# DRAM sums of the second FFN weights: half pieces on ScalarE's queue, one layer in the scan and one in attention; tile sums behind plain tiles

## The chip, the core and the metric

The kernel runs on one core of a Trainium2 chip. The metric is the device time of one execution in microseconds (us); where several runs are given, their median. A profile is of one execution; its times count from the start of its span.

## What is computed

One inference step of a two-layer encoder on 1024 prompt frames and 64 frames of a running stream, 1088 columns in all, in float32:

```python
for layer in range(2):
    if layer == 0:   # Mamba-2 mixer: in-projection, short convolution, scan over chunks, gate, out-projection
        m = ssd_mixer(rmsnorm(x, nw[0]), h0, c0, *params)
    else:            # banded attention on a shared K/V of the stream after layer 0
        k, v = shared_kv(x, kv_norm_w, w_kv)
        m = band_attention(rmsnorm(x, nw[0]) @ w_q, k, v, rel_bias) @ w_o
    x = x + rmsnorm(m, nw[1])
    x = x + rmsnorm(swiglu(rmsnorm(x, nw[2]), ffn_w_in[layer], ffn_w_out[layer]), nw[3])

def swiglu(u, w_in, w_out):
    g, up = split(u @ w_in, 2)          # 1024 -> 2 x 2816
    return (silu(g) * up) @ w_out       # 2816 -> 1024
```

Outputs are the stream, the scan's and convolution's states and the new K/V rows.

## The kernel before

**Numbers and products.** Each float32 operand is split into a high part (rounded to the format that TensorE takes) and a low part, and a product is made of three matmuls (L489 to L491, L1378 to L1380, L1714 to L1716). The high part is a ScalarE copy, the low part a VectorE subtraction (`part`, L363 and L364). For some weights, those planned with `acc`, the low part is made otherwise: ScalarE writes the negated high part (L358), and a DMA of GpSimd's queue adds the weights from DRAM (L359).

**Stages.** The scan (in-projection, convolution and chunk scan, up to about 690 us), out-projection, FFN of layer 0, attention, FFN of layer 1. The loops run over weight tiles of 128 x 1024 and three slices of columns, `SL` (384, 384, 320); in the FFN over two blocks of columns.

**FFN.** Both FFN products save multiplications by Strassen's scheme in Winograd's form: seven products of blocks stand for eight, and need sums of weight blocks. For the first weights the sums are made tile by tile, next to the work: SP loads a block into `tt` (L282), a DMA of GpSimd's queue adds a second one (L288, a "tile sum"), and VectorE finishes (L330, L331); `advance` does the planning. The first 6 tile pairs of each FFN (`PGS`) are plain, without sums; the first three and the last of these pairs are `acc` tiles. `sq` is the list of tiles still to be split, in order, and a tile with the key `two` is of the seven-product kind; `aq` holds tile sums that wait for their time.

**DRAM sums.** For the second weights the sums are made once, in DRAM, long ahead of use: `weight_sums(layer)` fills `wsm_[layer]`, of shape (128, 4, 4, 1408), from `w_f2[layer]`. With a and b the two weight tiles of group g (of four), each cut into halves of n = 1408 columns, a0, a1, b0, b1, it makes z[3] = b0 + b1 and z[2] = a0 + b0, z[0] = z[3] + a0 and z[1] = a1 + z[0], in five steps: copy into z[2:4], add, copy z[3] to z[0] and a1 to z[1], add, add. Copies are DMAs of SP's queue, adds are accumulating DMAs of GpSimd's queue, all from DRAM to DRAM. The two layers' steps are chained, 40 in all, and three are issued ahead of each group of units of the scan, from the fifth group on (L1157 to L1160). FFN of layer 0 loads the sums from about 1370 us on, FFN of layer 1 from about 2700 us on (L1322).

**What sets the order.** TensorE's order is the program's. All other engines' queues are ordered by a scheduler that looks at when it thinks an instruction is ready, and at priorities; each queue then runs in order on the chip. To keep an early transfer from being moved to the front, a manual dependency places it behind another instruction of the same engine: SP's copies behind the last weight load (`W.loaded`), the sums behind `last_g`, the last halo copy of a convolution on GpSimd (L826).

**The scan's inner work.** A "unit" is one product of a weight tile with a slice, 24 matmuls. `order` lists groups of two or three weight tiles (18 groups), each run over three slices. A unit's result is scaled out of PSUM by VectorE (L798), then goes through the convolution (`Conv`: ScalarE L836, VectorE L838, ScalarE L842 to L846) or a gate. `ssd_task` runs the chunk scan for one weight tile and slice: SP loads MT and ea, rows of the decay table spread over partitions (L922, L925); VectorE subtracts (L931), ScalarE takes the exponential (L932, L933).

**Attention.** For each of eight pairs of heads j there are nine units, K, V and Q for three slices (`evk`, `evv`, `evq`), which run ahead of nine blocks of scores. `load_bias(j)` loads two bias tiles and GpSimd masks their corners (L1809, L1810); there are three buffers, so the second tile of a pair waits for the first of the pair before. GpSimd also clears the ends of K (L1826), Q (L1845) and V (L1880); K has two buffers for each head. ScalarE copies K's high part (L1829), takes the softmax's exponentials (L1928) and empties every second transposed tile (L1948).

Of the kernel before, what the change touches and what calls it, by code (L numbers as in the profile page):

```python
# [2 lines left out]

# [87 lines left out]
C_CB = 168  # L91
# [144 lines left out]
class Weights:  # L236
# [38 lines left out]
    def advance(self):  # L275
        moved = True
        while moved:
            moved = False
            while self.tq and self.tt.free():
                it = self.tq.pop(0)  # L280
                it["T"] = self.tt.get()
                self.loaded = self.nc.sync.dma_start(it["T"].rearrange("p (e k) -> p e k", e=2), it["two"][0])  # L282
                if self.behind is not None:
                    self.tc.add_manual_dep(self.loaded.ins, self.behind.ins.name, ORDER, reason="place in the order")
                self.aq.append((self.clock() + ACC_W, it))
            while self.aq and self.aq[0][0] <= self.clock():
                it = self.aq.pop(0)[1]
                self.nc.gpsimd.dma_start(it["T"], it["two"][1], accum_op=ALU.add)  # L288
# [111 lines left out]
def hybrid_kernel(  # L400
# [63 lines left out]
    def col(c):  # L464
        return pcs[:, c:c + 1]
# [123 lines left out]
            UC.put(c)  # L589


    last_g = [None]

    def weight_sums(layer):

        w2, z, n = w_f2[layer], wsm_[layer], HF * P

        def sp(x):
            tc.add_manual_dep(x.ins, W.loaded.ins.name, ORDER, reason="place in the order")

        def pool(x):
            tc.add_manual_dep(x.ins, last_g[0].ins.name, ORDER, reason="place in the order")

        steps = []
        for g in range(4):
            a, b, to = w2[2 * g], w2[2 * g + 1], z[:, g]
            steps.append((
                lambda g=g, to=to: sp(nc.sync.dma_start(to[:, 2:4, :], w2[2 * g:2 * g + 2, :, :n].rearrange("e p k -> p e k"))),
                lambda b=b, to=to: pool(G.dma_start(to[:, 2:4, :], b.rearrange("p (e k) -> p e k", e=2), accum_op=ALU.add, max_dma_last_dim=4 * n)),
                lambda a=a, to=to: (sp(nc.sync.dma_start(to[:, 0, :], to[:, 3, :])), sp(nc.sync.dma_start(to[:, 1, :], a[:, n:]))),  # L610
                lambda a=a, to=to: pool(G.dma_start(to[:, 0, :], a[:, :n], accum_op=ALU.add)),
                lambda to=to: pool(G.dma_start(to[:, 1, :], to[:, 0, :], accum_op=ALU.add)),
            ))
        for f in range(5 + 3):
            for g in range(4):
                if 0 <= f - g < 5:
                    yield steps[g][f - g]

    order = []
    for g in range(NG):  # L620
# [94 lines left out]
    with ExitStack() as es:  # L715
# [92 lines left out]
        class Conv:  # L808
# [5 lines left out]
            def __call__(self, s, ps_):  # L814
                ct = self.ct
                dst = self.dst[s] = sb2.tile([P, 384], F32, tag=self.tag, bufs=self.bufs, name=self.tag)
                raw = sb2.tile([P, 390], F32, tag="craw", bufs=4, name="craw")
                if s == 0:
                    G.memset(raw[:, 0:3], 0.0)
                else:  # L820
                    G.tensor_copy(raw[:, 0:3], self.prev[:, 0:3])
                if s < 2:
                    w_ = 384
                    scaled(raw[:, 3:387], ps_, s, 0, 384)
                    self.prev = sb2.tile([P, 4], F32, tag="halo", bufs=5, name="halo")
                    last_g[0] = G.tensor_copy(self.prev[:, 0:3], raw[:, 384:387])  # L826
                else:
                    w_ = 323
                    G.tensor_copy(raw[:, 259:262], scs[:, ct, :])
                    scaled(raw[:, 3:259], ps_, s, 0, 256)  # L830
                    scaled(raw[:, 262:326], ps_, s, 256, 64)
                    G.tensor_copy(cst[:, ct, 0:3], raw[:, 256:259])
                    G.tensor_copy(cst[:, ct, 3:6], raw[:, 323:326])

                cw = C_CW + ct * 4
                A.activation(dst[:, :w_], raw[:, 0:w_], AF.Identity, bias=col(C_CB + ct), scale=col(cw))  # L836
                for k in range(1, 4):
# [316 lines left out]
            pend[s] = [dps] * (s < 2) + box  # L1154
        finish(2)
        side[0] = pyy
        staged = chain_of(weight_sums(0), weight_sums(1))  # L1157
        for i, grp in enumerate(order):
            for _ in range(3 if i > 3 else 0):
                next(staged, lambda: None)()  # L1160
            ws = [W.get() for _ in grp]
            ev = [evac_of(*f) for f in grp]
            if len(grp) < 3:
                seq = [(i, s) for s in range(NSL) for i in range(len(grp))]
                if grp is order[0]:

                    seq = [(0, 0), (0, 1), (1, 0), (1, 1), (1, 2), (0, 2)]
            else:
                seq = [(0, 0), (1, 0), (0, 1), (0, 2), (2, 0), (1, 1), (2, 1), (1, 2), (2, 2)]
            for i, s in seq:  # L1170
                kd_, jj_ = grp[i]
                q = 3 * jj_ + s
                if kd_ == "x":
                    st.wait_for(lambda: so["C"] > q - 5)
                elif kd_ == "z":
                    st.wait_for(lambda: so["D"] > q - 3)
                elif kd_ == "C" and q >= 5:
                    g_, s_ = divmod(q - 5, 3)
                    st.wait_for(lambda: so["C"] > 3 * (4 * g_ + 3) + s_)
                unit(ws[i], u[s], SL[s][1], lambda p_: ev[i](s, p_))  # L1180
                if s == 2:
                    W.put()
        nc.sync.dma_start(cst_o, cst)
# [588 lines left out]
    with ExitStack() as es:  # L1772
# [30 lines left out]
        def load_bias(j):  # L1803

            bias = []
            for e in range(2):
                bt = late["sb3"].tile([P, WIN], F32, tag="bias", bufs=3, name="bias")
                nc.sync.dma_start(bt, bass.AP(rbrow.tensor, (2 * j + e) * 768, [[1, P], [1, WIN]]))
                G.memset(bt[0:64, 0:64], NEG)  # L1809
                G.memset(bt[64:128, 576:640], NEG)  # L1810
                bias.append(bt)
            kqv[j]["bias"] = bias

        def evk(j):
            d = kqv[j]

            def f(s, p_):
                n = SL[s][1]
                st.wait_for(lambda: ("rb", s) in done)
                kf = sb2.tile([P, 384], F32, tag="kqv", bufs=2, name="kf")  # L1820
                with tc.high_priority(HIP):
                    V.tensor_tensor(kf[:, :n], p_[:, :n], rba[s][:, :n], op=ALU.mult)
                if not d["Kt"]:
                    d["Kt"] = [sb2.tile([P, 9 * P], F32R, tag=f"K{e}", bufs=2, name=f"K{e}") for e in range(2)]
                    for Kd in d["Kt"]:
                        G.memset(Kd[:, T:].bitcast(F32), 0.0)  # L1826
                for e, Kd in enumerate(d["Kt"]):
                    hi, lo = Kd[H2[e], 384 * s:384 * s + n], Kd[H2[1 - e], 384 * s:384 * s + n]
                    A.copy(hi, kf[H2[e], :n])  # L1829
                    V.tensor_tensor(lo, kf[H2[e], :n], hi, op=ALU.subtract)  # L1830
                d["K"].add(s)
                if s:
                    a_, b_, c_ = (128, 384, 0) if s == 1 else (0, 320, 256)
                    nc.sync.dma_start(kT_o[j * P:(j + 1) * P, c_:c_ + b_ - a_], kf[:, a_:b_])
# [237 lines left out]
        st.wait_for(lambda: cur["A"] >= 3)  # L2072
        units(wq, 0, evq, (2,))
        W.put()
        for j in range(1, 8):
            if j > 1:
                load_pair(j)
# [9 lines left out]
            while left:  # L2087
# [171 lines left out]
```

## Time and profile before

| | us |
|---|---|
| median of 3 runs | 2953.83 |
| lowest, highest | 2951.97, 2958.01 |
| the profiled execution | 2944.86 |
| its span, first to last instruction | 2943.2 |

| stretch of the profile (us) | length | TensorE busy | DMA share |
|---|---|---|---|
| 850 to 900 | 50 | 50.00 | 0.76 |
| 900 to 950 | 50 | 42.75 | 0.72 |
| 1600 to 1650 | 50 | 38.79 | 0.38 |
| 1700 to 1750 | 50 | 47.24 | 0.27 |
| 2250 to 2300 | 50 | 45.69 | 0.65 |
| 2400 to 2450 | 50 | 50.00 | 0.60 |

In the profile PE is TensorE, PEld its weight loads, DVE VectorE, ACT ScalarE, POOL GpSimd and SP the engine that issues most DMAs; a q behind a name is that engine's sequencer, which waits and issues DMAs. L with a number is a line of the kernel. A row of a timeline has the start, the duration, engine, line, operation, output and inputs, and in brackets how long the engine was idle before it and what ended that. A row of busy time by stretch has busy us and count of each engine, the mean granted clock of TensorE, the share of time that the 16 DMA engines were busy, and GB/s.

### The profile page before, as it was taken

What the parts mean: (1) busy time and instruction counts of PE and PEld (TensorE: products, weight loads), DVE (VectorE), ACT (ScalarE), POOL (GpSimd) and SP (SyncE); (2) the same over time, 40 slices, a digit from 0 to 9 for tenths busy, and PEclk for the clock granted to TensorE, in tenths of its full rate; (3) what the DMA queues carried; (4) which work ended last, traced back from release to release, by engine and by line L of the source; (5) the groups of instructions that cost most, each with busy time, mean ns of one, the idle gap of its engine ahead of it and who ended that gap; (6) DMA issues with size and microseconds to landing.
All of it is one profiled execution on the core that took longest, in us unless ns stands there. A gap on an engine that the chain in (4) does not pass through costs nothing. (4 is left out here: it accounts for less than half of the span.)

```text
span 2943.2 us, 58213 instructions
## 1 busy us (share of the span) xinstructions
PE 2858.4 (97%) x22094; PEld 2810.2 (95%) x22094; DVE 2131.8 (72%) x4834; ACT 1424.9 (48%) x2616; POOL 605.3 (21%) x880
## 2 busy tenths in 40 slices
PE   8999998999999999999999899999999999999999
PEld 8998898999998999999998899999999999999998
DVE  7987786886767665676559877877768766567567
ACT  6655545554554333344345556656565333334343
POOL 1334334340220222221022000000031122221011
PEclk9999999999999999999999999999999999999999
DMA  4439677654647656577655222222368555667666
GB/s 137 129 132 240 179 206 205 182 162 140 191 143 195 160 142 161 139 213 224 191 173 164 89 65 89 77 72 76 100 202 230 144 146 151 161 188 222 194 197 193
DMA packets 261673, 471.30 MB, mean 160 GB/s; under 512 B 26256, under 2 KB 162672, under 8 KB 261392
## 3 DMA queue, kind: packets, MB, share of 16 engines
q1 hardware_dynamic: 241584, 400.40, 42.0%
q0 software_dynamic: 19808, 67.19, 13.3%
q8 instruction: 173, 2.83, 0.4%
q14 instruction: 108, 0.88, 0.1%
HBM read 381.90 MB, written 127.26 MB: 173 GB/s over the span
## 5 line engine op out<-in xcount | busy, mean ns | idle before, releaser
L489 PE MATMUL mm<-r,hl 128*128 128x384 f32 (+2 forms) x1704 | 571.4, 335 | 25.2 <-DVE zs L798 12.4
L490 PE MATMUL mm<-r,hl 128*128 128x384 f32 (+2 forms) x1704 | 552.4, 324 | 2.4 <-DVE r L1592 2.4
L491 PE MATMUL mm<-r,hl 128*128 128x384 f32 (+2 forms) x1704 | 552.1, 324 | 1.4 <-DVE hl L364 0.7
L489 PEld LDWEIGHTS mm<-r,hl 128*128 128x128 f32 x1704 | 324.1, 190 | 31.6 <-DVE zs L798 12.6
L1379 PE MATMUL px<-r,hl 128*128 128x288 f32 (+1 forms) x1184 | 348.8, 295 | 0.0
L490 PEld LDWEIGHTS mm<-r,hl 128*128 128x128 f32 x1704 | 324.2, 190 | 3.3 <-DVE r L1592 3.0
L491 PEld LDWEIGHTS mm<-r,hl 128*128 128x128 f32 x1704 | 323.3, 190 | 2.0 <-DVE hl L364 1.1
L1380 PE MATMUL px<-r,hl 128*128 128x288 f32 x1056 | 313.3, 297 | 4.6 <-DVE hl L364 4.5
L1378 PE MATMUL px<-r,hl 128*128 128x288 f32 x1056 | 311.6, 295 | 0.0
L364 DVE TENSOR_TENSOR hl<-raw,hl 128x1024 fp32r<-128x1024 f32 (+2 forms) x171 | 195.1, 1141 | 92.9 <-ACT hl L363 92.3
L1714 PE MATMUL po<-r,hl 128*128 128x288 f32 (+1 forms) x856 | 246.7, 288 | 0.0
L1715 PE MATMUL po<-r,hl 128*128 128x288 f32 (+1 forms) x856 | 246.7, 288 | 0.0
L1716 PE MATMUL po<-r,hl 128*128 128x288 f32 (+1 forms) x856 | 246.6, 288 | 0.0
L1379 PEld LDWEIGHTS px<-r,hl 128*128 128x128 f32 x1184 | 223.7, 189 | 0.0
L363 ACT CAST hl<-raw 128x1024 fp32r<-128x1024 f32 (+2 forms) x171 | 165.7, 970 | 110.2 <-PE po L1716 41.4
L1378 PE MATMUL px<-rx,hl 128*128 128x256 f32 x768 | 213.8, 278 | 1.6 <-DVE u L1393 1.6
L1380 PE MATMUL px<-rx,hl 128*128 128x256 f32 x768 | 213.9, 279 | 0.3 <-DVE hl L364 0.3
L1380 PEld LDWEIGHTS px<-r,hl 128*128 128x128 f32 x1056 | 200.1, 189 | 5.4 <-DVE hl L364 5.3
L1378 PEld LDWEIGHTS px<-r,hl 128*128 128x128 f32 x1056 | 200.2, 190 | 0.0
L1379 PE MATMUL px<-rx,hl 128*128 128x256 f32 x640 | 178.3, 279 | 0.0
L1714 PEld LDWEIGHTS po<-r,hl 128*128 128x128 f32 x856 | 161.5, 189 | 0.0
L1716 PEld LDWEIGHTS po<-r,hl 128*128 128x128 f32 x856 | 160.9, 188 | 0.3 <-DVE hl L364 0.3
(385 smaller groups left out, 8019.2 us busy)
## 6 DMA issues: line engine op xcount, KB each, us to landing
raw<-in_w_f_dram SPq DMA_DIRECT2D x64, 512.0 KB, 4.9
tt<-in_w_f_dram SPq DMA_DIRECT2D x44, 512.0 KB, 4.1
tt<-in_w_f_dram POOLq DMA_DIRECT2D x44, 512.0 KB, 6.6
raw<-in_w_in_dram SPq DMA_DIRECT2D x40, 512.0 KB, 4.4
MT<-ascr SPq DMA_DIRECT2D x48, 384.0 KB, 4.9
raw<-in_w_so_dram SPq DMA_DIRECT2D x32, 512.0 KB, 3.8
r<-hscr SPq DMA_DIRECT2D x56, 288.0 KB, 3.9
wsum<-in_w_f_dram SPq DMA_DIRECT2D x8, 1408.0 KB, 10.1
```

The costliest lines, as they stand in the source:

```text
L363: self.nc.scalar.copy(h, v)
L364: (eng or self.eng or self.nc.vector).tensor_tensor(lo, v, h, op=ALU.subtract)
L489: PE.matmul(ps[:, :n], h_, xh, start=(first and i == 0), stop=False)
L490: PE.matmul(ps[:, :n], h_, xl, start=False, stop=False)
L491: PE.matmul(ps[:, :n], l_, xh, start=False, stop=(last and i == nk - 1))
L1378: PE.matmul(ps, wh, ah[:, k, :], start=(k == 0), stop=False)
L1379: PE.matmul(ps, wh, al[:, k, :], start=False, stop=False)
L1380: PE.matmul(ps, wl, ah[:, k, :], start=False, stop=(k == 3))
L1714: PE.matmul(ps, wh, xh, start=(k0 > 0 and i == ks[0]), stop=False)
L1715: PE.matmul(ps, wh, xl, start=False, stop=False)
L1716: PE.matmul(ps, wl, xh, start=False, stop=(k0 == 0 and i == ks[-1]))
```

## The change

The tile sums of `advance` are issued only when the next tile to be split is of the seven-product kind. `weight_sums` makes eight pieces for a layer, each half of a group's columns (704), in six steps; up to three pieces are in work in turn. The copies go out on ScalarE's queue, behind `last_a`: the last convolution's first instruction in the scan, the last copy of K's high part in attention. In the scan one step of layer 0's sums follows each unit of the first two slices, from the second group of units on; in attention one step of layer 1's sums follows each unit from j = 1 on, with the sums placed behind the last bias memset. The DRAM transfers' bytes stay the same in all.

```diff
-            while self.aq and self.aq[0][0] <= self.clock():
+            while self.aq and self.aq[0][0] <= self.clock() and 'two' in self.sq[0]:
                 it = self.aq.pop(0)[1]
                 self.nc.gpsimd.dma_start(it["T"], it["two"][1], accum_op=ALU.add)
...
-    last_g = [None]
+    last_g, last_a = [None], [None]
...
-        steps = []
-        for g in range(4):
-            a, b, to = w2[2 * g], w2[2 * g + 1], z[:, g]
-            steps.append((
-                lambda g=g, to=to: sp(nc.sync.dma_start(to[:, 2:4, :], w2[2 * g:2 * g + 2, :, :n].rearrange("e p k -> p e k"))),
-                lambda b=b, to=to: pool(G.dma_start(to[:, 2:4, :], b.rearrange("p (e k) -> p e k", e=2), accum_op=ALU.add, max_dma_last_dim=4 * n)),
-                lambda a=a, to=to: (sp(nc.sync.dma_start(to[:, 0, :], to[:, 3, :])), sp(nc.sync.dma_start(to[:, 1, :], a[:, n:]))),
-                lambda a=a, to=to: pool(G.dma_start(to[:, 0, :], a[:, :n], accum_op=ALU.add)),
-                lambda to=to: pool(G.dma_start(to[:, 1, :], to[:, 0, :], accum_op=ALU.add)),
-            ))
-        for f in range(5 + 3):
-            for g in range(4):
-                if 0 <= f - g < 5:
-                    yield steps[g][f - g]
+        c = n // 2
+
+        def behind(x, last):
+            tc.add_manual_dep(x.ins, last[0].ins.name, ORDER, reason="place in the order")
+
+        def copy(to, x):
+            behind(A.dma_start(to, x), last_a)
+
+        def add(to, x):
+            behind(G.dma_start(to, x, accum_op=ALU.add), last_g)
+
+        def steps(g, o):
+            a, b, to = w2[2 * g], w2[2 * g + 1], z[:, g, :, o:o + c]
+            yield lambda: copy(to[:, 2:4, :], w2[2 * g:2 * g + 2, :, o:o + c].rearrange("e p k -> p e k"))
+            yield lambda: add(to[:, 2:4, :], b.rearrange("p (e k) -> p e k", e=2)[:, :, o:o + c])
+            yield lambda: copy(to[:, 0, :], to[:, 3, :])
+            yield lambda: copy(to[:, 1, :], a[:, n + o:n + o + c])
+            yield lambda: add(to[:, 0, :], a[:, o:o + c])
+            yield lambda: add(to[:, 1, :], to[:, 0, :])
+
+        pieces = [steps(g, o) for g in range(4) for o in (0, c)]
+        live = []
+        while pieces or live:
+            while pieces and len(live) < 3:
+                live.append(pieces.pop(0))
+            for p_ in list(live):
+                f = next(p_, None)
+                if f is None:
+                    live.remove(p_)
+                else:
+                    yield f
...
-                A.activation(dst[:, :w_], raw[:, 0:w_], AF.Identity, bias=col(C_CB + ct), scale=col(cw))
+                last_a[0] = A.activation(dst[:, :w_], raw[:, 0:w_], AF.Identity, bias=col(C_CB + ct), scale=col(cw))
...
-        staged = chain_of(weight_sums(0), weight_sums(1))
-        for i, grp in enumerate(order):
-            for _ in range(3 if i > 3 else 0):
-                next(staged, lambda: None)()
+        staged = weight_sums(0)
+        for grp in order:
...
                 unit(ws[i], u[s], SL[s][1], lambda p_: ev[i](s, p_))
+                if s < 2 and grp is not order[0]:
+                    next(staged, lambda: None)()
...
-                G.memset(bt[64:128, 576:640], NEG)
+                last_g[0] = G.memset(bt[64:128, 576:640], NEG)
...
-                    A.copy(hi, kf[H2[e], :n])
+                    last_a[0] = A.copy(hi, kf[H2[e], :n])
...
+        staged = weight_sums(1)
         for j in range(1, 8):
...
                 units(ws[i], j, evs[i], (s,))
+                next(staged, lambda: None)()
```

More of the change, by code (lines that the diff above doesn't have):

```diff
@@ L1 @@
 from contextlib import ExitStack
-from itertools import chain as chain_of
 import concourse.bass as bass
@@ L589, in drop_u @@
             UC.put(c)
-    last_g = [None]
+    last_g, last_a = [None], [None]
     def weight_sums(layer):
         w2, z, n = w_f2[layer], wsm_[layer], HF * P
[L598 to L602, printed above, removed]
-        steps = []
-        for g in range(4):
-            a, b, to = w2[2 * g], w2[2 * g + 1], z[:, g]
-            steps.append((
[L608 to L611, printed above, removed]
-                lambda to=to: pool(G.dma_start(to[:, 1, :], to[:, 0, :], accum_op=ALU.add)),
-            ))
-        for f in range(5 + 3):
-            for g in range(4):
-                if 0 <= f - g < 5:
-                    yield steps[g][f - g]
```

## The prediction

> **What bounds the kernel now.** I read the page first, then busy time by stretches, then TensorE's waits in the one stretch that loses time, and from there back to what came late.
>
> ```profile
> span 2943.2 us, 58213 instructions
> PE 2858.4 (97%) x22094; PEld 2810.2 (95%) x22094; DVE 2131.8 (72%) x4834; ACT 1424.9 (48%) x2616; POOL 605.3 (21%) x880
> ```
>
> TensorE is the bound: it is idle for only 2943.2 - 2858.4 = 84.8 us, and no edit here takes a matmul away. So the change can win only idle time, and time under a lowered clock. The next view gives busy time by stretch: each pair is us and count; clock, DMA share and GB/s stand last.
>
> ```profile
> core 0: us, PE busy (x) PEld busy (x) DVE busy (x) ACT busy (x) POOL busy (x), PEclk, DMA share, GB/s
> 100.00:209.00 109.00, 108.80 (x778) 106.04 (x777) 98.87 (x244) 65.45 (x99) 47.51 (x73) 1.00 0.37 119
> 209.00:510.00 301.00, 279.21 (x1936) 269.85 (x1936) 226.98 (x582) 152.11 (x226) 120.14 (x184) 0.99 0.76 208
> 510.00:640.00 130.00, 130.00 (x917) 127.73 (x917) 108.31 (x277) 72.08 (x106) 51.29 (x86) 1.00 0.68 191
> ```
>
> These are three parts of the scan. Ahead of 209 us TensorE loses 0.2 us, after 510 us nothing, and between them 301.0 - 279.2 = 21.8 us, a quarter of all its idle time. The clock of 0.99 costs about 3 us more there. What begins at 209 us? The DRAM sums: their copies on SP's queue, with their starts, are these.
>
> ```profile
> L608 SPq DMA_DIRECT2D wsum<-in_w_f_dram x8: 596/614/708, 209.0 to 508.7; - x8
> L610 SPq DMA_DIRECT2D wsum<-wsum x8: 497/523/1101, 234.4 to 596.6; - x8
> L610 SPq DMA_DIRECT2D wsum<-in_w_f_dram x8: 588/590/1827, 235.6 to 597.1; - x8
> ```
>
> Durations are ns of the issuing instruction. How sums and stalls hang together is seen in TensorE's waits between 100 and 700 us (us in total, times, longest), and in the loads of MT (L922), first for 100 to 209 us, then for 209 to 510 us:
>
> ```profile
> PE mm L489 <- DVE zs L798: 12.4, 8, 7.0
> ```
> ```profile
> DMA to landing us min/median/max: 3.6/4.3/4.8
> ```
> ```profile
>   DVE MT L931: 36.3, 13
> DMA to landing us min/median/max: 4.0/6.8/15.0
> ```
>
> TensorE waits for VectorE to empty PSUM, and VectorE stands in its queue behind L931, whose MT hasn't landed. The worst place, by time (start, duration, wait in brackets):
>
> ```profile
> 444.44 1.17 POOL L609 DMA_DIRECT2D wsum<-in_w_f_dram  x1
> 451.01 0.84 POOL L611 DMA_DIRECT2D wsum<-in_w_f_dram  x1
> 458.93 1.20 DVE L931 TENSOR_SCALAR MT<-MT,nac 128x128 f32<-128x128 f32 x6 [9.53 <-DMA MT<-ascr]
> 460.65 0.64 PE L489 MATMUL mm<-r,hl 128*128 128x320 f32 x1 [7.01 <-DVE zs L798]
> ```
> ```profile
> 457.00:461.00 4.00, 0.34 (x1) 0.35 (x2) 1.67 (x7) 0.80 (x1) 0.00 (x0) 0.50 1.03 266
> ```
>
> Two sums go out on GpSimd, the DMA engines are full (share 1.03), VectorE waits 9.53 us, TensorE 7.01, and the clock falls to 0.50. Of 9.53 us VectorE's wait TensorE had about 2.5 covered: short waits cost nothing, long ones nearly all.
>
> **Scan: layer 0's sums alone, in halves.** One of the eight groups of before moves 2 x 1408 + 4 x 704 = 5632 KB, so both layers 45.1 MB, from 209.0 to about 610 us: 112 KB/us, and three copies may go out together. After, layer 0 alone makes 22.5 MB in 48 steps, one behind each unit with s < 2, four in a group of units. A group lasts about 401 / 13 = 30.9 us, so steps are 7.7 us apart, start near 209 - 3 x 30.9 = 116 us and last 12 groups, 371 us: 61 KB/us. Landing times bound what a half costs (KB each, median us to landing):
>
> ```profile
> wsum<-in_w_f_dram SPq DMA_DIRECT2D x8, 1408.0 KB, 10.1
> wsum<-in_w_f_dram POOLq DMA_DIRECT2D x8, 1408.0 KB, 11.2
> ...
> wsum<-in_w_f_dram SPq DMA_DIRECT2D x8, 704.0 KB, 7.8
> wsum<-in_w_f_dram POOLq DMA_DIRECT2D x8, 704.0 KB, 7.7
> ```
>
> From 1408 to 704 KB a sum falls from 11.2 to 7.7 us, not to half; on that line 352 KB take an estimated 6 us. So 48 steps of about 6.5 us are in flight for some 312 of 371 us: an MT load will meet a piece most of the time, but one half piece, hardly ever two or three whole ones. VectorE's 13 waits average 36.3 / 13 = 2.8 us; with about half of that each they fall under the cover of 2.5 us, all but a few. I leave 6 us of the 24.8 lost (21.8 + 3): **19 us won**. The ends are 24.8 (nothing lost, as after 510 us at a share of 0.68) and 0 (the halves delay MT as the wholes did; a rival below).
>
> The Trainium skill, "DMA: Bandwidth & Descriptors", section "Issuing engines are not separate DMA queues", says that transfers started from any engine run on the same 16 DMA engines and interleave, and that issuing from several saves only sequencer time. That speaks against a gain from ScalarE's queue as such. The trace agrees: the MT load that landed at 458.9 us stood beside sums of GpSimd's queue, not of SP's. By that rule the win is that of size and rate alone, which is how the 19 us are worked out; the queue adds none.
>
> **ScalarE's queue.** No DMA of before goes out on it, so SP's rows above are the nearest: 8 x (0.614 + 0.523 + 0.590) = 13.8 us for a layer's 24 copies if a half costs as much to issue as a whole (same count of rows), 6.9 if it goes by bytes; by each row's longest 8 x (0.708 + 1.101 + 1.827) = 29. ScalarE is idle for 301 - 152 = 149 us of the middle stretch, so most lies beside other work; what delays a conv or an exp comes through. I take 2 us of loss in the scan, between 0 and 13.8. The third copy of a piece needs its first sum; a piece's steps are three apart, 23 us, twice the 11.2 us that a whole one takes to land, so ScalarE should find it landed. SP is rid of the 13.8 us of issuing; TensorE waits for nothing of SP's in this stretch but MT, so that wins nothing by itself. GpSimd issues as many sums in the scan as before (24).
>
> **Attention: layer 1's sums.** Here TensorE has no idle time to give:
>
> ```profile
> 1750.00:2050.00 300.00, 299.98 (x2415) 291.27 (x2413) 235.17 (x741) 181.67 (x453) 8.53 (x55) 1.00 0.24 75
> ```
>
> GpSimd is nearly free (8.53 of 300 us), DMA at 0.24 takes 22.5 MB over some 48 x 6.8 = 330 us easily, but 13.8 us of issue come onto ScalarE (181.67 of 300 busy), whose exps and pT copies TensorE follows closely. I take a third, 4 to 5 us: **4 us lost**, between 0 and 13.8, waits apart. For the waits look at GpSimd's queue:
>
> ```profile
> 1825.18 0.15 POOL L1826 MEMSET K<- 128x64 f32 x1 [45.16 <-PE S L1914]
> ...
> 1829.94 0.15 POOL L1810 MEMSET bias<- 64x64 f32 x1
> ...
> 1886.66 0.15 POOL L1826 MEMSET K<- 128x64 f32 x1 [45.16 <-PE S L1914]
> ```
>
> A pair lasts 1886.66 - 1825.18 = 61.5 us, nine units, so a step comes each 6.8 us. A sum stands behind the last bias memset (L1810) of the pair being planned, whose bias buffer comes free only when the pair before is scored, after six of nine units. A sum of the first unit so waits 5 x 6.8 = 34 us. Counting steps (5 in j = 1, then 9 each), that meets the first sum of the third piece and of the sixth. The queue's order on GpSimd follows readiness, not the program (the K memset of a later pair stands ahead of a bias memset), so I expect the dependent copies to be placed late enough; a few us of mismatch are in the 4.
>
> **Tile sums behind plain tiles (start of each FFN).** TensorE waits there for the last plain tile's low part. Its sum is ready once L358 ends but stands behind a tile sum that waits for its own load:
>
> ```profile
> 931.42 1.07 ACT L358 ACTIVATE hl<-hl 128x1024 fp32r<-128x1024 f32 x1
> 937.51 0.88 POOL L288 DMA_DIRECT2D tt<-in_w_f_dram  x1 [9.93 <-DMA tt<-in_w_f_dram]
> 938.10 1.20 POOL L359 DMA_DIRECT2D hl<-in_w_f_dram  x1
> 943.06 0.69 DVE L330 TENSOR_TENSOR t<-tt,raw 128x512 f32<-128x512 f32 x1 [6.88 <-DMA tt<-in_w_f_dram]
> 947.26 0.58 PE L491 MATMUL mmx<-rx,hl 128*128 128x256 f32 x1 [6.13 <-DMA hl<-in_w_f_dram]
> 956.36 1.22 DVE L364 TENSOR_TENSOR hl<-tt,hl 128x1024 fp32r<-128x1024 f32 x1
> 958.76 0.41 DVE L1393 TENSOR_TENSOR u<-px,p 128x256 f32<-128x256 f32 x1
> ```
>
> Without it L359 goes at 932.5, 5.6 us sooner, and the stall of 6.13 nearly closes. But what is late next? L288 still waits for its load until 937.5, so VectorE still starts at 943.06 and works without a gap to 957.6, the end of the third split the first pair needs; P6's result was taken at 958.76. TensorE then waits there: about 1.3 us won. Layer 1 is the same:
>
> ```profile
> 2283.04 0.58 PE L491 MATMUL mmx<-rx,hl 128*128 128x256 f32 x1 [3.98 <-DMA hl<-in_w_f_dram]
> ...
> 2294.72 0.38 PE L1380 MATMUL px<-rx,hl 128*128 128x256 f32 x1 [0.32 <-DVE hl L364]
> ```
>
> TensorE already waits for VectorE at 2294.72, so some 0.3 us. Together **2 us won**; the ends are 0 and 6.1 + 4.0 = 10, if VectorE's order moves along.
>
> **Sum.** 19 - 2 - 4 + 2 = 15 us. The profiled execution took 2944.86 us (its span is 2943.2), so it would take 2930. The runs' median, 2953.83 (2951.97 to 2958.01), lies 9 us above it; taking the difference over gives 2938.8, rounded to **2939 us**.
>
> **Rivals.** (a) *MT is as late as before*: the pieces are in flight for most of the scan, and a half keeps the larger part of a whole's landing (7.7 of 11.2 us). Then the scan wins nothing, and -2 - 4 + 2 gives 2958; with half of the 19 won it is 2948; I write 2953. Against it: after 510 us sums still ran and TensorE lost nothing. The skill's page above, section "Bandwidth", has the rule that goes this way: batch to 1 MiB or more, since each transfer has a fixed cost; the two landing rows agree. (b) *ScalarE waits in attention (slower)*: if a dependent copy stands at its place in the program, it heads ScalarE's queue while its sum is held behind L1810: 34 - 20.4 (three steps) + 11.2 for landing = 25 us, twice; less some 2 us of cover each that is 46 us, and 2939 + 46 = 2985. It decides from about 8 us a copy. Against it: the order on GpSimd above. For it: ScalarE runs in order, and GpSimd waited 45 us in one place. (c) *All goes well*: the scan wins 24.8 - 1, the FFN starts 10, attention loses 1: 2921.
>
> **Chances.** Forecast 0.68, with a range of its own of 2927 to 2948; (a) 0.14; (b) 0.10; (c) 0.08. From 2926 to 2954 lie nearly all of the forecast's case and most of (a), some 0.8. A measurement of this kernel tells about 0.2%, 5.9 us, from no change. Faster: forecast and (c), 0.76; same: (a), 0.14; slower: (b), 0.10.
>
> **What would show it.** Right: between 116 and 500 us TensorE loses under 8 us, VectorE's waits for MT total under 15 us and no clock of 0.50 stands there; the copies are rows of ScalarE's queue of about 0.5 to 0.6 us; between 1750 and 2050 us TensorE loses under 6 us; L359 stands ahead of the first L288 and the stalls at 947 and 2283 us shrink, with VectorE named as the new wait. Wrong: waits of ScalarE for wsum of more than 5 us (b); MT landings with a median still near 6.8 us and stalls as many (a); a new stall in 116 to 209 us, where VectorE is busiest (98.87 of 109 us) and sums now run.

## The result, and the profile after

| | before | after |
|---|---|---|
| median of 5 runs each, side by side (us) | 2951.97 | 2969.64 |
| lowest, highest | 2940.31, 2958.01 | 2964.20, 2976.18 |
| span of the profiled execution | 2943.2 | 2974.5 |

The ratio of after to before is 1.0067, with a 95% interval of 1.0044 to 1.009: slower by about 20 us, where 15 us of gain were forecast. Of all the runs in this document one stands apart, one of e5's first six, which took 5465.81 us at a mean granted clock of 0.925; e5's median and ratio leave it out. The page's head of the changed kernel:

```profile
span 2974.5 us, 58300 instructions
PE 2875.0 (97%) x22094; PEld 2826.5 (95%) x22094; DVE 2132.4 (72%) x4834; ACT 1420.3 (48%) x2612; POOL 625.1 (21%) x904
```

TensorE runs as many matmuls as before, is idle for 2974.5 - 2875.0 = 99.5 us (84.8 before), and its matmuls take 16.6 us more: a lowered clock. Where? Busy time by stretch of the changed kernel, with the three stretches of the scan and one of attention that were read before:

```profile
100.00:209.00 109.00, 104.13 (x737) 101.20 (x734) 87.26 (x232) 55.77 (x83) 44.98 (x69) 0.96 0.62 176
209.00:510.00 301.00, 296.36 (x2076) 289.71 (x2074) 246.57 (x617) 167.80 (x251) 129.06 (x203) 0.99 0.58 153
510.00:640.00 130.00, 129.93 (x908) 127.62 (x904) 108.30 (x279) 69.76 (x106) 47.38 (x78) 1.00 0.32 102
...
1750.00:2050.00 300.00, 279.09 (x2167) 268.47 (x2161) 205.97 (x644) 157.00 (x394) 27.05 (x72) 0.95 0.47 125
```

The scan did in kind what was forecast: its middle stretch loses 4.6 us instead of 21.8, at the price of 4.9 us in the stretch ahead of it, where sums now run too. Attention, which lost 0.02 of 300 us, loses 20.9, at a clock of 0.95. The loads of MT took a median of 6.8 us and at the longest 15.0 between 209 and 510 us before; in the changed kernel they take:

```profile
DMA to landing us min/median/max: 3.6/4.8/7.5
```

A common ruler for all kernels: the starts of three TensorE waits that every one has (a row's start less its wait): at the scan's end (for VectorE's y), near attention's start (for vt), and at the second FFN's start (for hl). The last column is the difference of the two before it.

| kernel | scan's end | attention | second FFN | attention's length |
|---|---|---|---|---|
| before | 671.0 | 1626.9 | 2279.1 | 652.1 |
| after, first profile | 661.6 | 1617.0 | 2309.1 | 692.2 |
| after, second profile | 654.9 | 1611.4 | 2299.8 | 688.4 |

So by these profiles the changed kernel wins 9.4 to 16.1 us in the scan, carries them to attention, and loses 36 to 40 us there.

**What happens in attention.** Who waited for whom between 1690 and 2060 us in the changed kernel (us in total, times, longest):

```profile
PE S L1922 <- DVE pT L1957: 22.2, 8, 4.5
```
```profile
ACT Ck L1802 <- DMA cr<-in_ckT_dram: 16.2, 7, 4.0
ACT Qh L1860 <- DMA wsum<-in_w_f_dram: 15.3, 2, 7.7
...
ACT sc L1937 <- DMA wsum<-in_w_f_dram: 8.7, 1, 8.7
```

TensorE waits at its scores for VectorE, and ScalarE waits for two sorts of DMA: for sums (24.0 us in three waits) and for cr, the cached K rows of a pair (Ck is their split copy). One such place, GpSimd's timeline first:

```profile
1758.27 0.15 POOL L1835 MEMSET K<- 128x64 f32 x1 [45.38 <-PE S L1923]
...
1762.98 0.15 POOL L1819 MEMSET bias<- 64x64 f32 x1
1763.26 2.82 POOL L605 DMA_DIRECT2D wsum<-in_w_f_dram  x3
```

GpSimd stood 45.38 us at the head of its queue, waiting to clear a K buffer. Three sums stood behind it and behind the bias memset, and go out within 3 us. ScalarE, from the same moment (ACTq is its sequencer):

```profile
1773.42 0.48 ACTq L602 DMA_DIRECT2D wsum<-wsum  x1
1774.00 0.51 ACT L1860 CAST Qh<-qf 64x384 fp32r<-64x384 f32 x1 [7.58 <-DMA wsum<-in_w_f_dram]
...
1776.62 1.26 ACT L1802 CAST Ck<-cr 64x512 fp32r<-64x512 f32 x2
```

The copy from z[3] needs the first of the three sums and heads ScalarE's queue until it has landed; Qh, the high part of the queries, stands behind it, and ScalarE is idle for 7.58 us from 1766.4 on. VectorE and TensorE then:

```profile
1774.55 0.55 DVE L1862 TENSOR_TENSOR Ql<-qf,Qh 64x384 fp32r<-64x384 f32 x1 [6.44 <-ACT Qh L1860]
1775.02 0.28 DVE L1957 COPY pT<-ptp 128x128 f32<-128x128 f32 x1
```
```profile
1775.35 0.58 PE L1922 MATMUL S<-K,Qh 128*128 128x256 f32 x1 [4.35 <-DVE pT L1957]
```
```profile
1774.50:1781.30 6.80, 5.77 (x20) 5.47 (x21) 4.77 (x14) 5.29 (x16) 0.32 (x2) 0.50 0.72 220
```

VectorE's pT (a transposed tile that it empties), for which the scores wait, stands behind Ql, the queries' low part, Ql behind Qh, Qh behind a DRAM copy: 4.35 us of TensorE, and then 6.8 us at a clock of 0.50. The other thing that the pile delays are the loads of cr (KB each, median us to landing, 1690 to 2060 us), first of before, then of after:

```profile
cr<-in_ckT_dram SPq DMA_DIRECT2D x12, 128.0 KB, 2.5
```
```profile
cr<-in_ckT_dram SPq DMA_DIRECT2D x12, 128.0 KB, 8.0
```

In each of the six pairs of this stretch they are issued 1.2 to 2.5 us after the first of the sums let go at the bias memset (here at 1765.4 us, after 1763.26), so they always meet two or three sums. Two delays, then, with one release: ScalarE's head of the queue, and the pile beside the cache loads.

### The profile page after: what moved, and what is told of

It is laid out like the page before. It is cut to its first block, busy times and chain, and to the rows that moved or that the text cites. A ratio compares the mean times of both kernels' runs of the same rounds, so it can differ in the third digit from the quotient of the medians.

```text
span 2974.5 us, 58300 instructions
## 1 busy us (share of the span) xinstructions
PE 2875.0 (97%) x22094; PEld 2826.5 (95%) x22094; DVE 2132.4 (72%) x4834; ACT 1420.3 (48%) x2612; POOL 625.1 (21%) x904
## 5 line engine op out<-in xcount | busy, mean ns | idle before, releaser
L488 PEld LDWEIGHTS mm<-r,hl 128*128 128x128 f32 x1704 | 328.1, 193 | 19.4 <-DVE vt L1885 4.2
L489 PEld LDWEIGHTS mm<-r,hl 128*128 128x128 f32 x1704 | 328.0, 192 | 3.3 <-DVE r L1601 3.0
L490 PEld LDWEIGHTS mm<-r,hl 128*128 128x128 f32 x1704 | 327.1, 192 | 2.2 <-DMA hl<-in_w_in_dram 1.2
L1416 POOL TENSOR_TENSOR u<-u,c 128x256 f32<-128x256 f32 (+1 forms) x76 | 61.0, 802 | 487.1 <-DVE u L1414 401.6
L1723 PEld LDWEIGHTS po<-r,hl 128*128 128x128 f32 x856 | 161.5, 189 | 0.0
```

The costliest lines, as they stand in the source:

```text
L488: PE.matmul(ps[:, :n], h_, xh, start=(first and i == 0), stop=False)
L489: PE.matmul(ps[:, :n], h_, xl, start=False, stop=False)
L490: PE.matmul(ps[:, :n], l_, xh, start=False, stop=(last and i == nk - 1))
L1416: G.tensor_tensor(x["u3"], x["u3"], x["c22"], op=ALU.mult)
L1723: PE.matmul(ps, wh, xh, start=(k0 > 0 and i == ks[0]), stop=False)
```

## The experiments

Each is given with its edit, what was expected of it, and its ratio to before from runs side by side.

**e1: no hold in attention.** The bias memset no longer holds the sums:

```diff
-                last_g[0] = G.memset(bt[64:128, 576:640], NEG)
+                G.memset(bt[64:128, 576:640], NEG)
```

> Layer 1's sums lose their place behind the bias memset of GpSimd (L1819); the scan's last halo copy stays their only earlier instruction, and a sum then goes out when its own copy has landed. Theory A (the hold lets three sums pile up behind one memset, and the pile both keeps ScalarE's queue waiting and crowds the cache loads): the sums go out one by one, ScalarE's three waits of 7.4 to 8.7 us for a sum are gone or under 2 us, the stalls of TensorE on S fall from about 25 us to under 8 us, and attention ends about 10 us ahead of before as it began: 2935 to 2948 us. Theory B (any DRAM sum in attention costs this, held or not): the stalls stay at 20 us or more and the time at 2962 to 2972 us.

Measured: 2935.94 us, ratio 0.9969 (0.9956 to 0.9982). TensorE's waits at the scores between 1690 and 2060 us and the loads of cr:

```profile
PE S L1922 <- DVE pT L1957: 6.2, 3, 4.5
```
```profile
cr<-in_ckT_dram SPq DMA_DIRECT2D x12, 128.0 KB, 4.2
```

No wait of ScalarE for a sum is left, and attention takes 659.2 us. Theory A holds: the same sums, copies and queues cost some 30 us less when a single instruction no longer holds them together. The one wait of 4.5 us that stays is again at a pair's cr, with two sums beside it.

**e2: the dependent copy on GpSimd's queue.** The hold stays, ScalarE is freed of the copy that waits:

```diff
-            yield lambda: copy(to[:, 0, :], to[:, 3, :])
+            yield lambda: (behind(G.dma_start(to[:, 0, :], to[:, 3, :]), last_g) if layer else copy(to[:, 0, :], to[:, 3, :]))
```

> Layer 1's dependent copy (of the piece that has just been summed) is issued on GpSimd's queue in place of ScalarE's; the hold of the sums behind the bias memset stays. If ScalarE's wait at the head of its queue is the cause (theory A1), the waits of 7 to 9 us at Qh and sc go, the stalls that follow them (4.35, 4.52 and 3.1 us with their low clock) go with them, and the time is 2945 to 2955 us. If the burst of sums that crowds the cache loads is the cause (theory A2), the waits of ScalarE go but the stalls at Ck (waits of 3.7 to 4.0 us) stay, with 2960 to 2970 us.

Measured: 2960.85 us, ratio 1.005 (1.0035 to 1.0065), in theory A2's range. Waits of TensorE and ScalarE and the loads of cr between 1690 and 2060 us, and the place of the earlier example:

```profile
PE S L1922 <- DVE pT L1957: 18.2, 8, 4.1
```
```profile
ACT Ck L1802 <- DMA cr<-in_ckT_dram: 23.9, 11, 4.3
```
```profile
cr<-in_ckT_dram SPq DMA_DIRECT2D x12, 128.0 KB, 7.8
```
```profile
1764.06 0.62 ACT L1802 CAST Ck<-cr 64x512 fp32r<-64x512 f32 x1 [4.14 <-DMA cr<-in_ckT_dram]
```
```profile
1765.77 0.58 PE L1922 MATMUL S<-K,Qh 128*128 128x256 f32 x1 [3.87 <-DVE pT L1957]
```

ScalarE no longer waits for sums; the cast of Ck, which had come after that wait, now waits itself, and TensorE stands 3.87 us instead of 4.35. Attention's length is 679.3 us, 9 to 13 us under after's. The two delays lay side by side: taking one away uncovers most of the other. How the loss divides between them has no single answer; what is shown is that without the copy's wait some 27 us stay, and cr still lands late. GpSimd stands 25.6 us at the copies in their new place, but that is not what stays: nothing on TensorE or ScalarE waits for GpSimd in this stretch, and VectorE 2.8 us in all.

**e3: no sums of layer 1.** `weight_sums(1)` isn't run, and the second FFN reads layer 0's sums:

```diff
-                        src = wsm_[layer][:, g, y, k0 * P:(k0 + nk) * P]
+                        src = wsm_[0][:, g, y, k0 * P:(k0 + nk) * P]
...
-        staged = weight_sums(1)
+        staged = iter(())
```

> Layer 1's sums are left out, and layer 1's second weights are read from layer 0's sums. By the comparison of the two profiles the scan and layer 0 stand 10 to 11 us ahead of before and attention loses all: then attention takes what it takes in before, and the time is 2938 to 2946 us against 2952 us. If the rest of the change costs something in attention too (the tile sums, the tensors' places), the time stays above 2955 us.

Measured: 2935.63 us, ratio 0.9962 (0.9947 to 0.9977); attention 656.4 us. The time lies a little below the range that was expected. The whole loss is that of layer 1's sums, and the scan alone is worth 0.38%, 11 us of before's 2945.82 in that comparison. Against this kernel the runs give the loss another way: the ratios of the changed kernel, 1.0067 and below in a2 1.0076, stand 31 to 34 us above 0.9962, and e2's 1.005 stands 26 us above it.

**e5: the hold behind the memset of the query tiles.** Is it the pile, or its place? Here the piles stay, but start after the cache loads:

```diff
-                last_g[0] = G.memset(bt[64:128, 576:640], NEG)
+                G.memset(bt[64:128, 576:640], NEG)
...
-                        G.memset(q_[:, n:].bitcast(F32), 0.0)
+                        last_g[0] = G.memset(q_[:, n:].bitcast(F32), 0.0)
```

> Layer 1's sums are held behind GpSimd's memset of the query tiles (L1854) instead of the bias memset: the piles stay as large (three to six sums let go at once), but they start after the pair's cache loads have landed and not with them. Theory place (a pile costs because it runs beside the cache loads that ScalarE's Ck is waiting for): the loads of cr take under 5 us as in before, the stalls on S go, and attention takes 526 to 532 us from K to the FFN: 2934 to 2944 us. Theory pile (three sums at once cost wherever they stand, by ScalarE's wait for the dependent copy and by the other transfers): stalls of 3 to 5 us stay, in other places, at 2950 to 2970 us.

Measured: 2930.42 us, ratio 0.9942 (0.9923 to 0.9961), and in a second comparison 2932.27 us, 0.995 (0.9934 to 0.9965). GpSimd's timeline of the first, the loads of cr, TensorE's waits and attention's stretch:

```profile
1753.11 0.15 POOL L1819 MEMSET bias<- 64x64 f32 x1
...
1762.04 0.15 POOL L1854 MEMSET Ql<- 128x64 f32 x1
1762.40 1.88 POOL L605 DMA_DIRECT2D wsum<-in_w_f_dram  x2 [0.21 <-issue]
1763.48 1.64 POOL L605 DMA_DIRECT2D wsum<-wsum  x1
```
```profile
cr<-in_ckT_dram SPq DMA_DIRECT2D x13, 128.0 KB, 4.1
```
```profile
PE S L1922 <- DVE pT L1957: 2.6, 3, 1.7
```
```profile
1750.00:2050.00 300.00, 299.06 (x2413) 290.48 (x2411) 236.64 (x741) 183.10 (x453) 26.71 (x73) 1.00 0.51 133
```

Three sums still go out within 3 us, nine us later in the pair, and TensorE loses 0.9 of 300 us at a full clock. Attention takes 650.9 us, as before the change, with a DMA share of 0.51 instead of 0.24. Theory place holds, with a time even below its range: neither the bytes, nor ScalarE's 24 copies, nor a pile as such costs anything that can be seen here. ScalarE doesn't wait for a sum in this version either, so e5 takes both delays away at once; that the pile beside the cache loads is costly by itself is shown by e2, where it stays and the copy's wait is gone.

> Version e5 (layer 1's sums held behind the memset of the query tiles) once more, as the mate of the next three on this chip: ratio 0.992 to 0.996 to before again, 2925 to 2940 us, attention as long as in before to within 3 us.

**a2: the changed kernel once more.**

> The changed kernel once more, beside the others of this call. In its first profile the scan's end stood 9.4 us ahead of before; in those of e1, e2 and e3, which have the same scan, 16.3 to 16.5 us. If the difference is one of executions (stalls that fall a little longer and halve the clock, or don't), this profile shows 12 to 17 us, and attention loses 35 to 42 us again: 2958 to 2972 us. If the longer program of attention moved something in the scan, it shows 8 to 10 us again.

Measured: 2971.89 us, ratio 1.0076 (1.0061 to 1.009); the scan's end 16.1 us ahead of before, attention 688.4 us. So the 9.4 us of the first profile were that execution's, which had four short spells of low clock between 98 and 313 us where this one has one.

**e6: the scan on SyncE's queue.** Version e1, with layer 0's copies issued by SyncE:

```diff
-            behind(A.dma_start(to, x), last_a)
+            if layer:
+                behind(A.dma_start(to, x), last_a)
+            else:
+                behind(nc.sync.dma_start(to, x), [W.loaded])
```

> Version e1 (no hold in attention), with layer 0's copies issued on SyncE's queue behind the last weight load, as before the change did it, but in the new half pieces and new places. If the spread is what wins in the scan, nothing changes: the scan's end stays 15 to 17 us ahead, 2933 to 2941 us. If leaving SyncE's queue is what wins (a dependent copy that waits for its sum holds the weight loads behind it, as 7 us at 453.65 in before), 5 to 17 us are lost again: 2941 to 2953 us.

Measured: 2938.33 us, ratio 0.9966 (0.9955 to 0.9977), against 0.9969 of e1. The profile has the scan's end only 8.3 us ahead, in an execution with three spells of low clock between 98 and 313 us, much like after's first. By the runs the queue is worth nothing that can be measured. The 7 us at 453.65 of the expectation were TensorE's wait; SyncE's queue in before stood 4.1 us in all for sums, 3.2 at the longest.

**e10 and e11: how much in the scan is amount, how much is size.** The kernel before with layer 1's sums left out, so that layer 0's stand as before (the second FFN reads layer 0's, as in e3); and e5 with layer 0's sums in whole pieces:

```diff
-        staged = chain_of(weight_sums(0), weight_sums(1))
+        staged = weight_sums(0)
...
-                        src = wsm_[layer][:, g, y, k0 * P:(k0 + nk) * P]
+                        src = wsm_[0][:, g, y, k0 * P:(k0 + nk) * P]
```
```diff
-        c = n // 2
+        c = n // 2 if layer else n
...
-            behind(G.dma_start(to, x, accum_op=ALU.add), last_g)
+            behind(G.dma_start(to, x, accum_op=ALU.add, max_dma_last_dim=4 * n), last_g)
...
-        pieces = [steps(g, o) for g in range(4) for o in (0, c)]
+        pieces = [steps(g, o) for g in range(4) for o in ((0, c) if layer else (0,))]
```

> The kernel before, whose scan carries the sums of both layers, with layer 1's left out (layer 1's second weights are read from layer 0's sums): layer 0's stand as before in whole pieces, on SyncE's queue, three steps a group, from the fifth group on. Theory amount (the scan wins because half of its sums went elsewhere): the scan's end is 14 to 18 us ahead of before, the whole 2930 to 2938 us. Theory spread (it wins because pieces are half and places regular): the stalls at 250, 297, 325, 343 and 361 us stay, the scan's end is 2 to 8 us ahead, 2940 to 2948 us.

> Version e5 with layer 0's sums in whole pieces (24 steps of twice the bytes, in the same places from the second group on, done by the middle of the scan). Theory amount: no difference to e5 within 3 us. Theory spread: a sum of twice the bytes lies twice as long beside the loads, stalls grow in the first half of the scan, 4 to 10 us are lost: 2934 to 2941 us.

Measured: half the amount in before's manner gives 2935.95 us, ratio 0.9955 (0.994 to 0.9969), with the scan's end 10.1 us ahead in a profile of the longest of seven runs (2948.68 us). Whole pieces in the new places give 2955.77 us, 1.0024 (1.0009 to 1.0039), against 0.995 of e5 in the same comparison: some 22 us lost, far more than either theory's number. The stretch of 209 to 510 us of the first, that of 100 to 209 of the second, and the landing of MT in the latter:

```profile
209.00:510.00 301.00, 288.71 (x2021) 281.29 (x2020) 238.37 (x605) 159.07 (x240) 119.48 (x191) 0.99 0.61 173
```
```profile
100.00:209.00 109.00, 86.56 (x583) 83.67 (x583) 74.04 (x192) 48.63 (x72) 39.87 (x58) 0.87 0.71 199
```
```profile
DMA to landing us min/median/max: 3.9/11.1/18.0
```

With half the amount 12.3 us are still idle from 209 on: the stalls between 250 and 366 us stay, as theory spread had it, and those of 7.0 and 1.4 us at 460 and 495 us, beside layer 1's sums, are gone. The stretch ahead is whole again (108.58 of 109 us). The total is in theory amount's range and that of the half pieces alone (0.9955 beside e3's 0.9962); the scan's end lies between the two theories. Whole pieces that begin at 110 us stop TensorE for 22.4 of 109 us. So most of the scan's gain is the amount taken away, and a gain of the half pieces beyond it isn't seen in the runs. That whole pieces spoil the early start is shown, but in e11 the bytes per us double with the size, and which of the two does it isn't told apart.

**e8: a later start in the scan.** Version e5, with the sums beginning one group of tiles later:

```diff
-                if s < 2 and grp is not order[0]:
+                if s < 2 and grp not in order[:2]:
```

> Version e5 with layer 0's sums beginning one group of tiles later in the scan, so that none runs before about 130 us. If the stalls at 136 and 165 us (2.6 us each, which before doesn't have) come from sums beside the scan's densest loads, they shrink and 2 to 6 us are won: 2925 to 2929 us. If they come from ScalarE's and GpSimd's other new places, or move along with the sums, nothing is won: 2928 to 2935 us.

Measured: 2928.89 us, ratio 0.9937 (0.9923 to 0.9951), beside 0.995 (0.9934 to 0.9965) of e5. The waits at 136 and 165 us are gone, a new one of 2.7 us stands at 444 us. The medians are 3.4 us apart and the intervals overlap: the best version of this study, but not by a difference that is certain. It is faster than before and after.

**e4 and e7: the tile sums.** In both FFNs GpSimd's 104 tile sums and low parts stand in the same order in the traces of before and of after: the edit moved none of them. GpSimd's timeline of after at the first FFN:

```profile
925.42 0.85 POOL L287 DMA_DIRECT2D tt<-in_w_f_dram  x1 [9.25 <-DVE r L1232]
926.00 1.16 POOL L358 DMA_DIRECT2D hl<-in_w_f_dram  x1
```

The tile sum (L287) stands ahead of the plain tile's low part (L358), as before. So the place was given by a manual dependency, in both layers on the kernel before, and in layer 0 alone on e1 (`low` is the last L359 of a plain tile, L358 there; e4's edit is shown, e7's sets `low` in layer 0 only):

```diff
-            while self.aq and self.aq[0][0] <= self.clock():
+            while self.aq and self.aq[0][0] <= self.clock() and 'two' in self.sq[0]:
...
-                self.nc.gpsimd.dma_start(it["T"], it["two"][1], accum_op=ALU.add)
+                add = self.nc.gpsimd.dma_start(it["T"], it["two"][1], accum_op=ALU.add)
+                if self.low is not None:
+                    self.tc.add_manual_dep(add.ins, self.low.ins.name, ORDER, reason="place in the order")
+                    self.low = None
...
-            self.nc.gpsimd.dma_start(lo, acc, accum_op=ALU.add)
+            low = self.nc.gpsimd.dma_start(lo, acc, accum_op=ALU.add)
+            if ring is not self.half:
+                self.low = low
```

> The kernel before, with the one edit of the tile sums, and a fixed place for the first tile sum of each layer behind the low part of the last plain tile on GpSimd's queue, so that the step does what the prediction said it would. Theory by the prediction: the stall of TensorE on hl at the start of each FFN (6.1 and 4.0 us) shrinks by about 2 us net, 2950 us. Rival: the stall and the low clock behind it go wholly, 2940 to 2944 us. Rival: the summed tile is late in its place, no change or up to 4 us longer.

> Version e1 with the first tile sum of layer 0's FFN alone held behind the low part of the last plain tile. In e4 that took the stall on hl at the FFN's start from 6.1 to 2.1 us and stood 2.0 us better at 1290 us, while the same in layer 1 lost 15 us (a stall of 14.1 us). So the stall at 921 us falls from 6.2 to 2 us and the time by 2 to 5 us: 2930 to 2935 us. If the gain is lost with the summed tile later in layer 0, the time is that of e1, 2936 us.

Measured: both layers (e4) 2952.0 us, ratio 1.002 (1.001 to 1.003), slower; layer 0 alone (e7) 2935.36 us, 0.9953 (0.994 to 0.9967), against 0.9969 (0.9956 to 0.9982) of e1. TensorE's waits between 915 and 970 us, in e1 and with layer 0's order given:

```profile
PE mmx L490 <- DMA hl<-in_w_f_dram: 6.2, 1, 6.2
```
```profile
PE px L1395 <- DVE hl L369: 3.0, 2, 2.1
```

The wait for hl is gone, VectorE is the new one, 3.2 us less in all: the step as it was worked out in kind, with 1.3 us forecast for it. Yet from the scan's end to a late wait for hl of the first FFN that both have (1274.0 and 1277.2 us) the one took 619.4 us and the other 621.0. In these two profiles the gain is there, but in the FFN alone: from the last `nbp` matmul ahead of it (L551, at 905.6 us; L557, at 911.0) to that wait e1 took 368.4 us and e7 366.2. What hides it lies ahead: e7's profiled execution has two spells of low clock at 659 and 722 us and e1's none, and e7 took 3.8 us more up to that matmul. In layer 1 VectorE's order moved along; VectorE and TensorE there:

```profile
2296.11 5.15 DVE L1241 TENSOR_TENSOR r<-r 128x1152 fp32r<-128x1152 f32 x4
2301.19 1.21 DVE L369 TENSOR_TENSOR hl<-raw,hl 128x1024 fp32r<-128x1024 f32 x1
```
```profile
2302.45 0.58 PE L1385 MATMUL px<-rx,hl 128*128 128x256 f32 x1 [14.10 <-DVE hl L369]
```

Four splits of the data now stand ahead of a tile that TensorE waits for, and the stall of 4.0 us became one of 14.1.

The ruler of all of them:

| kernel | scan's end | attention | second FFN | attention's length |
|---|---|---|---|---|
| e1, no hold | 654.7 | 1609.8 | 2269.0 | 659.2 |
| e2, copy on GpSimd | 654.6 | 1612.2 | 2291.5 | 679.3 |
| e3, no sums of layer 1 | 654.5 | 1612.4 | 2268.8 | 656.4 |
| e5, hold behind Q | 655.8 | 1611.1 | 2262.0 | 650.9 |
| e5, again | 658.8 | 1618.0 | 2268.8 | 650.7 |
| e6, scan on SyncE | 662.7 | 1618.9 | 2277.2 | 658.3 |
| e10, half amount | 660.9 | 1618.9 | 2278.0 | 659.2 |
| e11, whole pieces | 680.1 | 1633.4 | 2285.5 | 652.1 |
| e8, later start | 653.8 | 1610.3 | 2260.3 | 650.0 |
| e7, order in layer 0 | 656.3 | 1612.8 | 2269.2 | 656.4 |
| e4, order in both layers | 670.2 | 1624.6 | 2276.2 | 651.6 |

Without any sum in attention it takes 651.6, 652.1, 656.4 and 659.2 us (e4, before, e3 and e10), so a difference of some 7 us in the last column is one of executions.

## Why the prediction was wrong

- **What bounds the kernel**: right. What was won and lost is idle time of TensorE and time at a lowered clock.
- **Scan, 19 - 2 us**: right in kind, too large by the runs. The profiles show 9.4 and 16.1 us; with attention's loss taken away the runs show 11 us (e3). MT's median fell from 6.8 to 4.8 us and VectorE's waits for it from 36.3 to 6.5 us between 209 and 510 us. The early stretch was costed at nothing and lost 4.9 and 4.0 us in the two profiles; it stood only among the warnings. VectorE's waits for MT there rose from 2.8 to 15.1 us. The split was off too: the amount does most of it, and no gain of the size alone is seen.
- **The queue adds none**, as the Trainium skill's "DMA: Bandwidth & Descriptors", section "Issuing engines are not separate DMA queues", has it: the runs agree (0.9966 beside 0.9969). A queue can lose by it all the same: in attention ScalarE's work stood 7.58 us behind one copy that had to wait.
- **ScalarE's issuing in attention, 4 us**: too large. In e5 all 24 copies are issued there and attention is as long as before.
- **The step that failed** stands in the attention part: "DMA at 0.24 takes 22.5 MB over some 48 x 6.8 = 330 us easily". It spread the transfers evenly and put what they do to other loads at nothing. But a hold also picks the moment of release: the sums stood behind the bias memset, that stood behind the K memset which waits 45 us, and two or three sums came out together just ahead of each pair's cache loads, whose landing rose from 2.5 to 8.0 us. With ScalarE's wait taken away, 26 of 31 to 34 us stay by the runs (e2); with the release moved off the cache loads the same sums cost nothing (e5). The row with the K memset's 45.16 us and the bias memset behind it were both quoted; the loads issued between them were not looked at.
- **The sentence on the copies failed too**: "so I expect the dependent copies to be placed late enough; a few us of mismatch are in the 4". The reason given for it, that GpSimd's order follows readiness and not the program, turned against it: the sums came out late, and the copies on ScalarE were not placed late enough, with three waits of 24.0 us in all.
- **Rival (b)** named this wait of ScalarE, its condition and its sign; 25 us twice became 7.6 to 8.7 us three times, just about the 8 us from which it was to decide. That the kernel came out slower as (b) said is in good part luck, since this wait is not the larger half of the cause.
- **Rival (a)**, MT as late as before: wrong for half pieces; with whole pieces and the early start it is what happens (median 11.1 us).
- **Tile sums, 2 us**: the edit moves nothing on GpSimd's queue. The prediction itself said that queues follow the scheduler's readiness, and didn't apply it here. With the order given by hand its working holds in kind in layer 0 (VectorE becomes the wait, 3.2 us less, 2.2 us over the FFN); in layer 1 the order of VectorE moves along, which was taken only as a chance of gain, and the stall grows to 14.1 us.

What stays open: how much of attention's loss is the one delay and how much the other, since they cover each other; and whether size or rate of the pieces spoils the early start of e11.

## What to carry to other kernels

An instruction that is held behind another on a queue that runs in order isn't only delayed: everything held comes out in one moment. Ask what the holder itself waits for, how much collects behind it, and which other transfers start at that moment; here another holder 9 us later in the same pair turned a loss of 0.7% into a gain of 0.5%. When two waits end close together, taking one away shows only the difference; find a change that takes both. And a place in the program is no place in a queue: look at the order on each engine before an edit of order is given a price.

## What the runs showed of the hardware

- A load of 128 KB that lands in 2.5 us (median) with little beside it took 8.0 us where two or three accumulating DRAM transfers of 352 and 704 KB went out just ahead of it on another queue, in most pairs with one or two DRAM copies; it took 4.0 us where two copies of 352 KB alone ran beside it (e5, at 1752.9 us).
- Sums of the same size land later when they start together with loads and copies: 704 KB took a median of 11.9 us in attention after the change and 7.4 us behind the query memset:

```profile
wsum<-in_w_f_dram POOLq DMA_DIRECT2D x8, 704.0 KB, 11.9
```
```profile
wsum<-in_w_f_dram POOLq DMA_DIRECT2D x7, 704.0 KB, 7.4
```

- The clock adds to the price of a stall: the wait of 4.35 us was followed by 6.8 us at 0.50, half of which is lost. A shorter wait can do it too, here one of 1.92 us in the scan of the changed kernel, with the stretch behind the clock's change and the one ahead of it:

```profile
168.99 0.42 PE L488 MATMUL mm<-r,hl 128*128 128x320 f32 x1 [1.92 <-DVE craw L807]
```
```profile
170.30:173.70 3.40, 3.40 (x16) 3.40 (x16) 3.40 (x10) 1.75 (x2) 0.02 (x1) 0.50 0.80 250
166.90:170.30 3.40, 1.48 (x10) 1.31 (x10) 3.40 (x10) 2.39 (x5) 1.24 (x5) 1.00 0.02 7
```

The Trainium skill, "TensorE: Matmul & The Clock Gate", section "What's actually happening", says that the clock goes to half after at least one idle window of about 3.4 us, and that the windows run freely. Here TensorE was busy for 1.48 of the 3.40 us ahead of the half rate, so a stretch that is idle for a little over half was enough, and the measurement decides; the slow stretch then lasts 3.4 us, and 6.8 after the wait of 4.35 us. Length alone doesn't decide: in the second profile a wait of 2.62 us at the same place, which ends at 166.98 us, was followed by no lower clock.
